# Softmax minus one-hot over 8192 rows: six in-place f32 row buffers, moved as two-row blocks in partition halves

## The chip, the core and the metric

The kernel runs on one core of one Trainium2 chip. The metric is the device time of one execution in microseconds. TensorE (PE) hardly takes part; the work is done by ScalarE (ACT), VectorE (DVE), a little by GpSimd (POOL), and by the core's 16 DMA engines, for which SyncE (SP) and ACT issue the large transfers.

## The reference

For each of 8 x 1024 = 8192 rows of 8192 logits: the softmax, from which 1 is taken away at the row's label.

```python
logits_max = np.max(logits, axis=-1, keepdims=True)
exp_logits = np.exp(logits - logits_max)
softmax = exp_logits / np.sum(exp_logits, axis=-1, keepdims=True)
one_hot[batch_idx, seq_idx, labels] = 1.0
return (softmax - one_hot).astype(np.float32)
```

Logits and result are f32, 268.4 MB each, so 537 MB cross between HBM and SBUF. The labels reach the kernel as 8-byte integers.

## The kernel before, in words

The rows are cut into 64 tiles of 128 rows, one row in each partition: 32 KB per partition, 4.194 MB per tile. The single loop runs over the tiles; the order of instructions on each engine follows the loop, and each instruction waits for its data by semaphores that the framework places.

Line 41 makes a constant of the column numbers 0 to 8191 as int16 on POOL. Then, for each tile:

- Line 47: SP issues the load of the tile into `logits_tile`. There are four such buffers, so the load of tile t has to wait until the store of tile t-4 has been read out of the same buffer.
- Line 50: POOL issues the load of the 128 labels, one per partition. Line 57: DVE turns them into f32.
- Line 61: ACT computes the exponential of the tile into `exp_bf` (bf16, two buffers). The row maximum isn't subtracted. The row sum is accumulated in the same pass.
- Line 71: DVE takes the reciprocal of the sum.
- Line 74: DVE compares the column numbers with the label and multiplies by the sum. The result, bf16, overwrites the first half of the logits' buffer.
- Line 83: DVE subtracts that from the exponentials.
- Line 85: DVE multiplies by the reciprocal and writes the f32 result over the tile's buffer.
- Line 87: ACT issues the store of the tile from that buffer.

Of the kernel before, what the change touches and what calls it, by code (L numbers as in the profile page):

```python
# [1 line left out]

# [4 lines left out]

P = 128


@with_exitstack
def kernel(
    ctx: ExitStack,
    tc: tile.TileContext,
    logits: bass.AP,
    labels: bass.AP,
    out: bass.AP,
):
    nc = tc.nc  # L20
    fp32 = mybir.dt.float32
    bf16 = mybir.dt.bfloat16
    i16 = mybir.dt.int16

    logits_nv = logits.flatten_outer_dims()
    out_nv = out.flatten_outer_dims()
    labels_n = labels
    while len(labels_n.shape) > 1:
        labels_n = labels_n.rearrange("a b ... -> (a b) ...")

    N, V = logits_nv.shape
    assert N % P == 0, f"N={N} must be a multiple of {P}"
    n_tiles = N // P

    const_pool = ctx.enter_context(tc.tile_pool(name="const", bufs=1))
    io_pool = ctx.enter_context(tc.tile_pool(name="io", bufs=4))
    work_pool = ctx.enter_context(tc.tile_pool(name="work", bufs=2))
    stats_pool = ctx.enter_context(tc.tile_pool(name="stats", bufs=4))

    iota_pv = const_pool.tile([P, V], i16)  # L40
    nc.gpsimd.iota(iota_pv[:, :], [[1, V]], channel_multiplier=0)  # L41

    for ti in range(n_tiles):
        rs = ti * P

        logits_tile = io_pool.tile([P, V], fp32, tag="io")
        nc.sync.dma_start(out=logits_tile[:], in_=logits_nv[rs : rs + P, :])  # L47

        labels_tile = stats_pool.tile([P, 1], labels_n.dtype, tag="labels")
        nc.gpsimd.dma_start(out=labels_tile[:], in_=labels_n[rs : rs + P, None])  # L50

        labels_f32 = stats_pool.tile([P, 1], fp32, tag="labels_f32")
        if mybir.dt.size(labels_n.dtype) == 8:
            labels_i32 = labels_tile.bitcast(mybir.dt.int32)[:, :1]
        else:
            labels_i32 = labels_tile[:]
        nc.vector.tensor_copy(out=labels_f32[:], in_=labels_i32)  # L57

        exp_bf = work_pool.tile([P, V], bf16, tag="exp")
        sum_f32 = stats_pool.tile([P, 1], fp32, tag="sum")  # L60
        nc.scalar.activation(  # L61
            out=exp_bf[:],
            in_=logits_tile[:],
            func=mybir.ActivationFunctionType.Exp,
            bias=0.0,
            scale=1.0,
            accum_out=sum_f32[:],
        )

        recip_sum = stats_pool.tile([P, 1], fp32, tag="recip")  # L70
        nc.vector.reciprocal(out=recip_sum[:], in_=sum_f32[:])  # L71

        ohts_bf = logits_tile.bitcast(bf16)[:, :V]
        nc.vector.tensor_scalar(  # L74
            out=ohts_bf,
            in0=iota_pv[:, :],
            scalar1=labels_f32[:],
            scalar2=sum_f32[:],
            op0=mybir.AluOpType.is_equal,
            op1=mybir.AluOpType.mult,  # L80
        )

        nc.vector.tensor_sub(out=exp_bf[:], in0=exp_bf[:], in1=ohts_bf)  # L83

        nc.vector.tensor_scalar_mul(out=logits_tile[:], in0=exp_bf[:], scalar1=recip_sum[:])  # L85

        nc.scalar.dma_start(out=out_nv[rs : rs + P, :], in_=logits_tile[:])  # L87


# [1 line left out]
_INS = ['logits', 'labels']  # L91
_OUTS = [((8, 1024, 8192), 'float32')]


# [23 lines left out]
```

## Time and profile before

| | us |
|---|---|
| median of 8 runs | 1255.51 |
| lowest and highest | 1254.31, 1257.36 |
| the profiled execution | 1257.36 |
| its span in the profile | 1255.5 |
| DVE busy | 732.6 |
| ACT busy | 457.0 |
| POOL busy | 253.0 |
| load, median from issue to landing | 29.1 |
| store, median from issue to landing | 29.4 |

The span runs from the first instruction to the last event that the profile holds. Busy time is the time in which an engine executes an instruction; the issuing of a DMA is not counted in it, so SP has none. "SPq" and "ACTq" name an engine's sequencer as it issues DMAs. In the groups of instructions, the part before the bar gives the operation, what it writes and reads with the shapes, and how often; after the bar stand the total busy time in us, the mean of one in ns, and the idle time of the engine just before these instructions with what ended it. Landing is the moment at which a transfer's completion is signalled.

### The profile page before, as it was taken

How to read it: one execution, taken by the hardware profiler on the slowest of the kernel's cores; microseconds unless marked ns; L12 is line 12 of the kernel's file. 1: busy time of each engine (PE TensorE's matmuls, PEld its weight loads, DVE VectorE, ACT ScalarE, POOL GpSimd, SP SyncE). 2: the span in 40 equal slices, each digit the busy share in tenths (PEclk: the TensorE clock that was granted, in tenths of full speed). 3: DMA queues.
4: the chain of work that ended last, by engine and by line, in shares of the span. 5: the costliest groups of instructions: out<-in, count | busy, mean ns of one | idle time of the engine just before them, and what ended most of it. 6: DMA issues, size and time to landing. Idle time of an engine off the chain costs nothing.

```text
span 1255.5 us, 992 instructions
## 1 busy us (share of the span) xinstructions
DVE 732.6 (58%) x320; ACT 457.0 (36%) x129; POOL 253.0 (20%) x69
## 2 busy tenths in 40 slices
DVE  3764655646547456465564654746647556465573
ACT  4424244243342433424324334243342432423422
POOL 5312212212122121221221212212122122100000
DMA  9999999999999999999999999999999999999996
GB/s 399 421 431 434 434 434 433 432 434 433 433 432 428 433 434 433 434 433 433 430 434 432 434 433 426 434 434 434 433 433 432 433 433 433 432 432 430 432 434 276
DMA packets 20487, 537.01 MB, mean 428 GB/s; under 512 B 4096, under 2 KB 4096, under 8 KB 4096
## 3 DMA queue, kind: packets, MB, share of 16 engines
q1 hardware_dynamic: 9216, 268.44, 49.7%
q10 hardware_dynamic: 9216, 268.44, 49.5%
q0 software_dynamic: 2048, 0.07, 0.1%
q14 instruction: 7, 0.06, 0.0%
HBM read 268.50 MB, written 268.44 MB: 428 GB/s over the span
## 4 chain that ended last, share of the span: by engine, by line
DMA 73%; DVE 14%; issue 11%; POOL 1%; ACTq 1%; ACT 0%; SPq 0%; PEldq 0%
DMA logits_tile<-in_logits_dram 46%; DMA out_dram<-logits_tile 26%; DVE logits_tile L85 5%; DVE exp_bf L83 5%; DVE logits_tile L74 4%; DMA labels_tile<-in_labels_dram 1%; POOL iota_pv L41 1%; ACTq L87 1%; ACT exp_bf L61 0%; POOL labels_tile L50 0%; DVE recip_sum L71 0%; DVE labels_f L57 0%; ACTq L61 0%; SPq L47 0%; PEldq L113 0%
## 5 line engine op out<-in xcount | busy, mean ns | idle before, releaser
L61 ACT ACTIVATE exp_bf<-logits_tile 128x8192 bf16<-128x8192 f32 x64 | 449.8, 7029 | 774.2 <-DMA logits_tile<-in_logits_dram 760.7
L50 POOL DMA_DIRECT2D labels_tile<-in_labels_dram x64 | 245.9, 3843 | 834.8 <-DVE labels_f L57 832.8
L71 DVE RECIPROCAL recip_sum<-sum_f 128x1 f32<-128x1 f32 x64 | 10.5, 163 | 488.0 <-ACT exp_bf L61 488.0
L85 DVE TENSOR_SCALAR logits_tile<-exp_bf,recip_sum 128x8192 f32<-128x8192 bf16 x64 | 287.1, 4486 | 0.1
L83 DVE TENSOR_TENSOR exp_bf<-exp_bf,logits_tile 128x8192 bf16<-128x8192 bf16 x64 | 283.2, 4425 | 2.2
L74 DVE TENSOR_SCALAR logits_tile<-iota_pv,labels_f,sum_f 128x8192 bf16<-128x8192 int16 x64 | 154.3, 2411 | 0.3 <-issue 0.3
L57 DVE CAST labels_f<-labels_tile 128x1 f32<-128x1 int32 x64 | 9.4, 147 | 20.2 <-DMA labels_tile<-in_labels_dram 20.2
L61 ACT ACTIVATION_READ_ACCUMULATOR exp_bf<-logits_tile 128x1 f32 x64 | 11.9, 186 | 0.0
L41 POOL IOTA iota_pv<- 128x8192 int16 x1 | 6.9, 6943 | 0.4 <-PEq L113 0.4
L61 ACT ACT_TABLE_LOAD x1 | 1.3, 1283 | 0.7 <-PEq L102 0.7
L102 POOL MEMSET const-float32-0.0<- 128x1 f32 x1 | 0.1, 99 | 0.2 <-issue 0.2
L102 POOL MEMSET const-bfloat16-1.0<- 128x1 bf16 x1 | 0.1, 102 | 0.0
L102 POOL MEMSET const-uint8-127<- 128x1 uint8 x1 | 0.1, 102 | 0.0
L102 POOL MEMSET const-float32-1.0<- 128x1 f32 x1 | 0.1, 99 | 0.0
## 6 DMA issues: line engine op xcount, KB each, us to landing
logits_tile<-in_logits_dram SPq DMA_DIRECT2D x64, 4096.0 KB, 29.1
out_dram<-logits_tile ACTq DMA_DIRECT2D x64, 4096.0 KB, 29.4
labels_tile<-in_labels_dram POOLq DMA_DIRECT2D x64, 1.0 KB, 12.8
```

The lines of the kernel that those rows point to most:

```text
L41: nc.gpsimd.iota(iota_pv[:, :], [[1, V]], channel_multiplier=0)
L50: nc.gpsimd.dma_start(out=labels_tile[:], in_=labels_n[rs : rs + P, None])
L57: nc.vector.tensor_copy(out=labels_f32[:], in_=labels_i32)
L61: nc.scalar.activation(out=exp_bf[:], in_=logits_tile[:], func=mybir.ActivationFunctionType.Exp, bias=0.0, scale=1.0, accum_out=sum_f32[:],)
L71: nc.vector.reciprocal(out=recip_sum[:], in_=sum_f32[:])
L74: nc.vector.tensor_scalar(out=ohts_bf, in0=iota_pv[:, :], scalar1=labels_f32[:], scalar2=sum_f32[:], op0=mybir.AluOpType.is_equal, op1=myb ...
L83: nc.vector.tensor_sub(out=exp_bf[:], in0=exp_bf[:], in1=ohts_bf)
L85: nc.vector.tensor_scalar_mul(out=logits_tile[:], in0=exp_bf[:], scalar1=recip_sum[:])
L87: nc.scalar.dma_start(out=out_nv[rs : rs + P, :], in_=logits_tile[:])
L102: nc = _bacc.Bacc("TRN2", target_bir_lowering=False, num_devices=1)
```

## The change

All six row buffers are one f32 tile `X` of three slots with two rows each. A block is 256 rows; partition p holds the rows 2p and 2p+1 of it, which lie next to each other in HBM, so that 64 KB per partition are one run. `rows` moves one of the two rows of all 128 partitions (32 KB each); `halves` moves both rows of 64 partitions (64 KB each). Both kinds have 4.194 MB. Loads of the blocks 0 to 4 and 27 to 31 and stores of the blocks 0, 1 and 24 to 31 go by rows, the others by halves.

The arithmetic stays in place in `X`: DVE finds the negated row maximum, ACT writes the exponential in f32 over the logits with the maximum as its bias, DVE takes the reciprocal of the sum, ACT scales the row by it, and DVE compares the column numbers with the label and subtracts, in one pass. The bf16 buffers are gone. The column numbers are made by POOL in the last row buffer and copied by DVE to PSUM. All labels are loaded at once, converted, and transposed by PE so that each partition has its own.

The order is written out by hand (`manual_schedule`): each engine runs its instructions as the text has them. For row t that is: exponential of t (ACT), reciprocal of t (DVE), load of the next block where t+1 opens one (SP), maximum of t+1 (DVE), store of t-1 (issued by ACT), scaling of t (ACT), subtraction of t (DVE). The last row's scaling and subtraction are cut into two column halves.

The diff, cut to its core:

```diff
+SLOTS = 3
+G = 2
+Q = P // 2
...
+    lab_bp = labels.rearrange("a b -> (a b)").rearrange("(b q) -> b q", q=G * P)
+    x_b = x_nv.rearrange("(b p j) v -> b p j v", p=P, j=G)
+    o_b = o_nv.rearrange("(b p j) v -> b p j v", p=P, j=G)
...
+    X = const.tile([P, SLOTS, G, V], fp32)
+    rows = [(slice(0, P), slice(j, j + 1)) for j in range(G)]
+    halves = [(slice(0, Q), slice(0, G)), (slice(Q, P), slice(0, G))]
...
+    nc.scalar.dma_start(out=lab_raw[:], in_=lab_bp)
...
+    nc.vector.tensor_copy(out=lab_f[:], in_=lab32[:, :, :, 0])
...
+            nc.tensor.transpose(out=lab_ps[:, j, :], in_=lab_f[:, j, :], identity=ident[:])
+        nc.vector.tensor_copy(out=lab[:], in_=lab_ps[:])
...
+    made = X[:, SLOTS - 1, G - 1, :].bitcast(i16)[:, :V]
+    nc.gpsimd.iota(made, [[1, V]], base=0, channel_multiplier=0)
+    nc.vector.tensor_scalar(
+        out=iota[:].bitcast(i32), in0=made.bitcast(i32), scalar1=0, scalar2=None, op0=Alu.bitwise_or
+    )
...
+    def parts(b, head, tail):
+        return rows if b < head or b >= B - tail else halves
+
+    def load(b):
+        for ps, js in parts(b, 5, 5):
+            nc.sync.dma_start(out=X[ps, b % SLOTS, js, :], in_=x_b[b, ps, js, :])
...
+    def row_max(t):
+        nc.vector.tensor_reduce(
+            out=m[:, t : t + 1], in_=row(t), axis=mybir.AxisListType.X, op=Alu.max, negate=True
         )
...
-        nc.vector.tensor_sub(out=exp_bf[:], in0=exp_bf[:], in1=ohts_bf)
+    def exponent(t):
+        nc.scalar.activation(
+            out=row(t), in_=row(t), func=Act.Exp, bias=m[:, t : t + 1], scale=1.0,
+            accum_out=s[:, t : t + 1],
+        )
...
-        nc.vector.tensor_scalar_mul(out=logits_tile[:], in0=exp_bf[:], scalar1=recip_sum[:])
+    def normalize(t, c):
+        x = row(t)[:, c]
+        nc.scalar.activation(out=x, in_=x, func=Act.Copy, bias=0.0, scale=r[:, t : t + 1])
...
+    def subtract(t, c):
+        x = row(t)[:, c]
+        nc.vector.scalar_tensor_tensor(
+            out=x, in0=iota[:, c], scalar=lab[:, t % G, t // G : t // G + 1], in1=x,
+            op0=Alu.is_equal, op1=Alu.subtract, reverse1=True,
+        )
...
+    def store(t):
+        b, j = divmod(t, G)
+        pieces = parts(b, 2, 8)
+        if pieces is rows:
+            pieces = rows[j : j + 1]
+        elif j < G - 1:
+            return
+        for ps, js in pieces:
+            nc.scalar.dma_start(out=o_b[b, ps, js, :], in_=X[ps, b % SLOTS, js, :])
...
+    load(0)
+    row_max(0)
+    for t in range(T):
+        exponent(t)
+        inverse(t)
+        if t + 1 < T:
+            if (t + 1) % G == 0:
+                load((t + 1) // G)
+            row_max(t + 1)
+        if t > 0:
+            store(t - 1)
...
+        for c in cols:
+            normalize(t, c)
+        for c in cols:
+            subtract(t, c)
+    store(T - 1)
```

## The prediction

> **What bounds the kernel now.** I read the page's slices first, then its queues and groups, then the waits, then the two ends.
>
> ```profile
> span 1255.5 us, 992 instructions
> DVE 732.6 (58%) x320; ACT 457.0 (36%) x129; POOL 253.0 (20%) x69
> DMA  9999999999999999999999999999999999999996
> ...
> q1 hardware_dynamic: 9216, 268.44, 49.7%
> q10 hardware_dynamic: 9216, 268.44, 49.5%
> ```
>
> No engine is above 58%, while the DMA engines are full in 39 of 40 slices. Loads (q1) and stores (q10) take half each. The windows of the trace give the rate and the two ends (columns: stretch, length, busy time of DVE, ACT, POOL, clock, DMA share, GB/s):
>
> ```profile
> 0.00:60.00 60.00, 32.12 (x19) 29.66 (x9) 23.26 (x16) 1.00 0.98 410
> 60.00:1200.00 1140.00, 672.96 (x293) 413.09 (x116) 229.76 (x54) 1.00 1.00 433
> 1200.00:1224.84 24.84, 16.07 (x6) 7.13 (x3) 0.00 (x0) 1.00 0.99 427
> 1224.84:1255.50 30.66, 11.41 (x4) 7.12 (x2) 0.00 (x0) 1.00 0.65 278
> ```
>
> I take 433.5 GB/s for the middle (the page's slices say 432 to 434). A tile of 4.194 MB then takes 9.68 us, and 128 of them (64 in, 64 out) 1239 us. The remaining 16.5 us are the start (410 instead of 433.5 over 60 us: 3 us), the end (278 over 30.7 us: 11 us) and small dips. So only some 16 us can be won while the bytes stay the same; much more can be lost.
>
> The waits of the loading queue say what a load waits for, and the groups what an operation costs:
>
> ```profile
> SPq L47 <- DMA out_dram<-logits_tile: 1170.1, 60, 50.1
> ```
> ```profile
> L61 ACT ACTIVATE exp_bf<-logits_tile 128x8192 bf16<-128x8192 f32 x64 | 449.8, 7029 | 774.2 <-DMA logits_tile<-in_logits_dram 760.7
> L71 DVE RECIPROCAL recip_sum<-sum_f 128x1 f32<-128x1 f32 x64 | 10.5, 163 | 488.0 <-ACT exp_bf L61 488.0
> L83 DVE TENSOR_TENSOR exp_bf<-exp_bf,logits_tile 128x8192 bf16<-128x8192 bf16 x64 | 283.2, 4425 | 2.2
> ```
>
> 60 of 64 loads wait for a store to free their buffer. ACT waits for loads, DVE for ACT. The ends, in order of time:
>
> ```profile
> 13.14 7.03 ACT L61 ACTIVATE exp_bf<-logits_tile 128x8192 bf16<-128x8192 f32 x1 [11.12 <-DMA logits_tile<-in_logits_dram]
> ...
> 23.35 7.03 ACT L61 ACTIVATE exp_bf<-logits_tile 128x8192 bf16<-128x8192 f32 x1 [3.09 <-DMA logits_tile<-in_logits_dram]
> ```
> ```profile
> 1238.98 4.49 DVE L85 TENSOR_SCALAR logits_tile<-exp_bf,recip_sum 128x8192 f32<-128x8192 bf16 x1
> 1243.50 0.34 ACTq L87 DMA_DIRECT2D out_dram<-logits_tile  x1
> ```
>
> The first tile lands at 13.1. The last store is issued at 1243.5 and the span ends 12.0 us later: 9.7 us of bytes and **2.3 us fixed** per transfer.
>
> **What the Trainium skill says.**
> - "SBUF — State Buffer", Door 1: DMA bandwidth depends on how many of 16 ports the partitions reach; partitions 0 to 63 reach eight (196 GB/s measured there for 1 MiB, asymptote about 218; all 128 reach sixteen). All transfers of the trace before span 128 partitions, so it doesn't test this; its 433.5 fits sixteen ports.
> - "DMA: Bandwidth & Descriptors", rules for kernel authors: transfers to two partition halves serialize. Not tested here either.
> - "VectorE: DVE Perf Modes", tier table and errata: an fp32 two-source operation and a reduction run at one element per cycle, (N+151)/0.96 ns. The trace agrees where it can: L83, at two per cycle, should be (4096+151)/0.96 = 4424 ns; it is 4425.
>
> **The change, part by part** (R a row tile, B a block of two rows).
>
> *Engine work.* Out go L74, L83 and L85 (11.3 us of DVE per tile), L57 and 64 label DMAs on POOL. Per row come a maximum and a compare-subtract on DVE, each (8192+151)/0.96 = 8.69 us by the price above (PSUM as a source could add some 0.1), and L71's 0.16: 17.55 us, 64 times 1123 us, 88% of a span. ACT has an exponential (L61's 7.03 plus the 0.18 readout, 7.3 with a tensor as bias) and a scaling copy of about 7.1: 14.4 us, 922 in all. A row of DMA pairs takes 19.35 us, so neither engine is the bound: they hide under DMA by 1.8 us per row, and show at the ends.
>
> *Set-up.* The labels' DMA, conversion, two transposes and the iota's copy to PSUM stand ahead of the first maximum on DVE. POOL's iota is 6.9 us (L41); the copy is 4096 words, about 4.4 us: ready near 13, when row 0 lands. Cost 0 to 2 us on DVE, hidden since DMA has six free rows to load. ACT's small load ahead of the big ones: under 0.5 us.
>
> *Order of issue.* On DVE, the subtraction of t stands behind the maximum of t+1. In half mode, a block's store therefore goes out only after the next block's landing L: 8.69 + 8.69 + 0.1 = 17.5 us later. The store's wait sits on ACT ahead of the scaling of t; ACT is free at 16.1, waits 1.4 us and has the copy done by 25.4, just before DVE asks for it (26.2): covered by 0.8 us; without the cover that is what DVE would lose.
>
> *Half mode* is what decides: blocks 5 to 26 are loaded and 2 to 23 stored as halves of 64 partitions, 4.194 MB each. With three slots, load b+2 needs the slot of store b-1, half for half. From the landing of b to that of b+2: 17.5 (store issued) + 2.3 + h (first half stored) + 0.1 + 2.3 + 2h (two halves loaded in sequence) = 22.2 + 3h, two periods long. At 218 GB/s, h = 19.24, so a period is **40.0 us**. The DMA sum alone would be 4 x 9.68 = 38.7; equality is at h = 18.4 (228 GB/s). h isn't in the trace. Bounds: 9.68 (no limit, then the period is 38.7, no less as the sum binds) and 21.4 (196 GB/s, period 43.2). I take 19.24, because the fixed part is already counted.
>
> *Walk.* Row 0 lands at 13.1; maximum to 21.8, exponential to 29.1, then DVE runs on: subtraction of t ends at 46.7 + 17.55t. DMA is full with 10 row loads and 4 row stores (135.5 us + 2.7 of start) to about 137. The store of block 2 goes out at 134.5, alone; load 5 may start when its first half lands: 134.5+2.3+19.2 = 156, and lands at 156.1+2.3+38.5 = **197**. Load 6 follows in the queue: 235.4. Then pairs of 79.9: L26 = 235.4 + 10 x 79.9 = **1034.6**. From there all is in rows: 10 loads and 14.7 row stores remain, 24.7 x 9.68 = 239 us + 0.7 for the receipt: **1274**. DVE gives 1270 for the same end (subtractions every 17.55 from 1052, the last row in halves, 12.0 for its store), so DMA is late and DVE next.
>
> Span 1274 against 1255.5: +18.5. The profiled execution took 1257.36, 1.86 more than its span and 1.85 above the median of 1255.51; so that execution would become 1276, and the median **1274**.
>
> **The rivals.**
> 1. *The port limit doesn't bite, and DMA stays full.* For it: 433.5 GB/s is reached with both directions mixed, and half loads and half stores overlap most of the time. Against: 3 us of each direction per period run alone, and the skill's figure. If a half runs at 228 GB/s or more, the period is 38.7. Then 1239 + 3 (start) + 2 (the gap near 135) + the end. After the last landing stand maximum 8.7, subtraction 8.7, half a copy 3.7, two half subtractions 8.9 and the store 12.0, 42.7 us with gaps, before 30.7; waiting stores fill 29 to 39 of it, so 4 to 14 are lost: 1248 to 1258, likeliest **1250**: faster. It decides from 228 GB/s per half upward.
> 2. *The halves wait for more than their half*, or two DMA engines on one port get in each other's way so that directions don't overlap. If a load's half waits for both halves of the store, the loop is 22.2 + 4h, a period of 49.6: 21 x 9.6 = 202 more, **1476**. For it: all six rows are one tile. Against: load and store divide it alike.
> 3. *DVE becomes the bound.* Needs over 19.35 us per row against 17.55; each operation would have to be 0.9 us longer. 64 x 19.5 + 29 = 1277: folded into my case.
>
> **How the numbers follow.** My case, with h from 18.8 to 21.4 us: 0.52, from 1262 to 1274 + 21 x 3.2 = 1341. Rival 1: 0.30, of which 0.21 faster, 0.08 within 0.2% (1253 to 1258), 0.01 slower. Rival 2 and like trouble: 0.18, above the range. Range 1247 to 1341; the likeliest case's own 1262 to 1341. Measurement tells 0.2% from no change. Faster 0.21, same 0.08, slower 0.71.
>
> **What would show it.** DVE at 1120 to 1135 us busy, groups of 8.7 us; half transfers of about 21 us or more from issue to landing when alone, and a slice near 140 to 160 us at about 218 GB/s; 415 to 420 GB/s between 200 and 1030 us; ACT and DVE idle on loads, SP's queue on stores; rows at the end at 433. Wrong: 433 GB/s throughout the middle, or a slice in which one half alone moves faster than 230.

## The result, and the profile after

The changed kernel takes **1699.74 us** (median of 11 runs, 1689.49 to 1733.11) against 1255.32 for the kernel before: 1.353 times as long, 95% interval 1.351 to 1.356. The run of 1733.11 us, over 1.5% above the fastest, counts as slow; ratio and interval are of the fast runs alone. The forecast was 1274, with a range up to 1341: the sign was right, the size far off. The profiled execution has a span of 1710.4 us.

First the page's slices and queues of the changed kernel:

```profile
span 1710.4 us, 746 instructions
...
DMA  9999999999999999999999999999999999999998
GB/s 408 428 431 303 284 279 276 290 264 265 317 253 282 296 302 268 279 279 285 268 285 282 291 280 299 291 280 280 297 277 285 293 274 273 403 431 435 433 432 379
...
q1 hardware_dynamic: 6400, 268.44, 57.3%
q10 hardware_dynamic: 6448, 268.51, 41.7%
```

Both kernels show a row of nines for the DMA engines. But the line below it says that full engines now move some 280 GB/s in slices 4 to 34, where they moved 433 before. The slices at both ends, where everything goes by rows, are as fast as ever. So the DMA engines hardly lack work; their packets take longer. The page also says how much longer. A packet is one run, the contiguous bytes of one partition: by 20 loads in rows (2560 packets of 32 KB), 44 loads in halves (2816 of 64 KB) and 16 completions per transfer, q1's 6400 packets are accounted for. 57.3% of 16 x 1710.4 us is 15,681 us; 2560 row packets at 1.22 us (before: 49.7% of 16 x 1255.5 over 8192) take 3,120; the rest over 2816 is **4.46 us per 64 KB load packet, where two row packets take 2.44**. The same sum for the stores gives **2.95 us**. Together 7.41 us for 2 x 64 KB, on 16 engines 283 GB/s.

The windows of the same trace (columns: stretch, length, busy time of PE twice, DVE, ACT and POOL, then clock, DMA share, GB/s) set the stretches apart:

```profile
0.00:140.00 140.00, 0.39 (x2) 0.28 (x2) 124.92 (x24) 99.90 (x22) 7.43 (x7) 1.00 1.00 420
140.00:200.00 60.00, 0.00 (x0) 0.00 (x0) 45.43 (x9) 44.63 (x10) 0.00 (x0) 1.00 1.02 283
200.00:1400.00 1200.00, 0.00 (x0) 0.00 (x0) 695.89 (x120) 571.80 (x120) 0.00 (x0) 1.00 0.99 282
1500.00:1600.00 100.00, 0.00 (x0) 0.00 (x0) 100.00 (x19) 82.37 (x17) 0.00 (x0) 1.00 1.00 434
```

The fall comes soon after 140 us; the first store in halves was issued at 133.37. In the middle DVE is busy 58% of the time. The groups and waits:

```profile
L94 DVE TENSOR_REDUCE m<-X 128x1 f32<-128x8192 f32 x64 | 555.2, 8674 | 491.3 <-DMA X<-in_logits_dram 491.3
L99 ACT ACTIVATE X<-X,m 128x8192 f32<-128x8192 f32 x64 | 455.5, 7118 | 557.8 <-DVE m L94 557.8
L113 DVE SCALAR_TENSOR_TENSOR X<-iota,lab,X 128x8192 f32<-128x8192 int16 (+1 forms) x65 | 559.7, 8612 | 71.3 <-ACT X L109 71.3
L109 ACT ACTIVATE X<-X,r 128x8192 f32<-128x8192 f32 (+1 forms) x65 | 456.0, 7016 | 202.3 <-issue 129.7
```

The work that was added costs what it was said to cost (8.67 us for a maximum, 8.74 for a full-width subtraction in the timeline, 7.12 for a copy). DVE waits 491 us for loads, in 26 places.

### The profile page after: what moved, and what is told of

Read it like the earlier page. It is cut to its first block, busy times and chain, and to the rows that moved or that the text cites. A ratio compares the mean times of both kernels' runs of the same rounds, so it can differ in the third digit from the quotient of the medians.

```text
span 1710.4 us, 746 instructions
## 1 busy us (share of the span) xinstructions
PE 0.4 (0%) x2; PEld 0.3 (0%) x2; DVE 1118.1 (65%) x196; ACT 917.2 (54%) x194; POOL 7.4 (0%) x7
## 3 DMA queue, kind: packets, MB, share of 16 engines
q1 hardware_dynamic: 6400, 268.44, 57.3%
## 4 chain that ended last, share of the span: by engine, by line
DMA 52%; DVE 26%; another core or an unknown queue 19%; issue 1%; ACT 1%; SPq 0%; DVEq 0%; PE 0%; ACTq 0%
DMA out_dram<-X 26%; DMA X<-in_logits_dram 25%; DVE m L94 13%; DVE X L113 12%; ACT X L99 0%; DMA lab_raw<-in_labels_dram 0%; SPq L88 0%; DVE iota L76 0%; DVEq L174 0%; ACT X L109 0%; DVE r L105 0%; DVE lab_f L62 0%; DVEq L94 0%; PE lab_ps L67 0%
## 5 line engine op out<-in xcount | busy, mean ns | idle before, releaser
L94 DVE TENSOR_REDUCE m<-X 128x1 f32<-128x8192 f32 x64 | 555.2, 8674 | 491.3 <-DMA X<-in_logits_dram 491.3
L99 ACT ACTIVATE X<-X,m 128x8192 f32<-128x8192 f32 x64 | 455.5, 7118 | 557.8 <-DVE m L94 557.8
L113 DVE SCALAR_TENSOR_TENSOR X<-iota,lab,X 128x8192 f32<-128x8192 int16 (+1 forms) x65 | 559.7, 8612 | 71.3 <-ACT X L109 71.3
L109 ACT ACTIVATE X<-X,r 128x8192 f32<-128x8192 f32 (+1 forms) x65 | 456.0, 7016 | 202.3 <-issue 129.7
L105 DVE RECIPROCAL r<-s 128x1 f32<-128x1 f32 x64 | 9.7, 152 | 7.3 <-ACT X L99 7.3
L99 ACT ACTIVATION_READ_ACCUMULATOR X<-X,m 128x1 f32 x64 | 11.9, 187 | 0.0
L75 POOL IOTA X<- 128x8192 int16 x1 | 6.9, 6943 | 0.0
L76 DVE TENSOR_SCALAR iota<-X 128x4096 int32<-128x4096 int32 x1 | 4.4, 4427 | 0.1
```

Source lines behind the costliest of these rows:

```text
L75: nc.gpsimd.iota(made, [[1, V]], base=0, channel_multiplier=0)
L76: nc.vector.tensor_scalar(out=iota[:].bitcast(i32), in0=made.bitcast(i32), scalar1=0, scalar2=None, op0=Alu.bitwise_or)
L94: nc.vector.tensor_reduce(out=m[:, t : t + 1], in_=row(t), axis=mybir.AxisListType.X, op=Alu.max, negate=True)
L99: nc.scalar.activation(out=row(t), in_=row(t), func=Act.Exp, bias=m[:, t : t + 1], scale=1.0, accum_out=s[:, t : t + 1],)
L105: nc.vector.reciprocal(out=r[:, t : t + 1], in_=s[:, t : t + 1])
L109: nc.scalar.activation(out=x, in_=x, func=Act.Copy, bias=0.0, scale=r[:, t : t + 1])
```

## Experiments

Three theories were open. The **port theory** takes up the ports that the prediction cites: partitions 0 to 63 lie behind eight of sixteen, two DMA engines share one, and when both move the same way each gets half. The **run-length theory**: a 64 KB run is slow by itself. The **loop theory**: three slots keep the DMA short of work.

### Transfers alone

These kernels compute nothing; each stage loads into or stores from `X`, and a tiny DVE write to every buffer (`gap`) parts the stages. Each was run once. Two of the twelve stages; `LO` is partitions 0 to 63, `MID` 32 to 95, both in 64 KB runs:

```diff
...
+    for slot in range(SLOTS):
+        load(LO, slot)
+    gap()
+    for slot in range(SLOTS):
+        load(MID, slot)
+    gap()
...
```

> Transfers alone, no arithmetic: twelve stages of loads and stores of 64 partitions or 128, with a gap after each; nothing is computed, so the output is only data moved from the logits. Port theory (partitions 0 to 63 lie behind eight of the sixteen ports, so two DMA engines share one): loads of 0 to 63 alone at 215 to 218 GB/s, of 32 to 95, with the same bytes and the same 64 KB runs, at about 430; halves in turn on one queue 218, on two queues between 218 and 430; stores likewise; load beside store of halves 260 to 300 in all, of 32 to 95 about 433. Run-length theory (a 64 KB run is slow by itself): 0 to 63 and 32 to 95 and the 128-partition blocks are all equally slow, at 280 or below, and only the 32 KB rows reach 430. Loop theory (the three slots starve the DMA): every stage here is at 400 or above, since nothing waits.

The gaps in the timeline of this run part the stages. The wait in brackets before a gap is the length of its stage (the first load was issued at 0.73, so the first stage took 60.7):

```profile
61.42 0.06 DVE L66 MEMSET X<- 128x6 f32 x1 [61.42 <-DMA X<-in_logits_dram]
122.14 0.06 DVE L66 MEMSET X<- 128x6 f32 x1 [60.66 <-DMA X<-in_logits_dram]
186.21 0.06 DVE L66 MEMSET X<- 128x6 f32 x1 [64.01 <-DMA X<-in_logits_dram]
218.27 0.06 DVE L66 MEMSET X<- 128x6 f32 x1 [32.00 <-DMA X<-in_logits_dram]
342.91 0.06 DVE L66 MEMSET X<- 128x6 f32 x1 [124.58 <-DMA X<-in_logits_dram]
...
463.40 0.06 DVE L66 MEMSET X<- 128x6 f32 x1 [120.43 <-DMA X<-in_logits_dram]
```

Below, the prediction's 2.3 us are taken off each length for what isn't bytes.

| stage | MB | us | GB/s |
|---|---|---|---|
| loads, rows of all partitions | 25.2 | 60.7 | 431 |
| loads, 64 KB runs, all partitions | 25.2 | 60.7 | 431 |
| loads, 0 to 63 | 12.6 | 64.0 | 204 |
| loads, 32 to 95 | 12.6 | 32.0 | 424 |
| loads, both halves in turn, one queue | 25.2 | 124.6 | 206 |
| loads, both halves at once, two queues | 25.2 | 120.4 | 213 |
| stores, 0 to 63 | 12.6 | 63.2 | 207 |
| stores, 32 to 95 | 12.6 | 31.0 | 438 |
| load 0 to 63 beside store 64 to 127 | 25.2 | 89.5 | 289 |
| load beside store, both 0 to 63 | 16.8 | 61.1 | 285 |
| load beside store, both 32 to 95 | 16.8 | 52.4 | 335 |
| load beside store, rows of all partitions | 33.6 | 81.1 | 426 |

The third and fourth lines decide: same bytes, same number of partitions, same runs, each transfer one contiguous stretch of HBM, and a factor of two from where the partitions lie. It isn't the number of engines at work either: the DMA share is full in both stages.

```profile
125.00:183.00 58.00, 0.00 (x0) 0.00 (x0) 1.00 0.97 199
190.00:216.00 26.00, 0.00 (x0) 0.00 (x0) 1.00 1.02 444
```

Two more lines say how it works. Both halves at once on two queues reach all ports between them, and still get 213 GB/s. In this stage's trace (344 to 461 us) all packets in flight belong to one of the two queues for 82% of the time: the engines go through both queues in step, most of the time all on one half, then all on the other. And load beside store gives 285 to 289 GB/s, more than the 204 of one direction, and whether the two use the same half or opposite ones makes no difference. So directions that differ get in each other's way less than transfers in the same direction. How much less can't be read against the 426 of the last line: 32 to 95, without shared ports, gave 335 beside a store, where 433 was expected. The halves alone came out a little below the expected 215 to 218.

A second run of this kind:

> Transfers alone again, eleven stages with a gap after each; nothing is computed, the output is only data moved. Port theory (engines that share a port and move the same way each get half of it): loads of partitions 0 to 63 in 32 KB rows at 205 to 215 GB/s as with 64 KB; every second partition at 215 to 430, as the two engines that meet on a port stay together or not; 0 to 31 at about 200; 0 to 15 (four engines on one port) at about 105; 64 KB blocks of all partitions, load beside store, 425 to 435; 32 to 95 load beside store in 64 KB 430 if the 335 of the first look came from its short stage, below 390 if something else is shared there; 0 to 63 load beside store in 32 KB rows again 260 to 310; halves in loads alone beside blocks in stores about 290 while both run, halves in stores alone 290 to 390. Run-length theory: the 32 KB stages are the fast ones.

Loads of 0 to 63 in 32 KB rows took 64.0 us for 12.6 MB (204 GB/s), of every second partition 32.0 us (424), of 0 to 31 33.0 us for 6.3 MB (205), of 0 to 15 21.3 us for 2.1 MB (110). So the number of partitions doesn't set the rate: 16, 32, 64 and again 64 partitions give 110, 205, 204 and 424, which fits the ports. Load beside store of 64 KB blocks of all partitions gave only 338 (101.5 us for 33.6 MB), of 32 to 95 in 64 KB 336, in 32 KB rows 395, of 0 to 63 in 32 KB rows 305. Halves in loads alone, beside whole blocks in stores, gave 322 GB/s, halves in stores alone 365. The 338 and 336 were not foreseen, and led to a third run:

> Loads beside stores alone, no arithmetic, all data only moved; runs cut to 64, 32, 8 and 2 KB on the HBM side, first for all partitions, then (32, 8, 2 KB) for 0 to 63, then every second partition in 64 KB runs. If the length of a run sets what two directions on one engine cost each other: all partitions 338 to 350 GB/s at 64 KB and 425 or more at 32 KB and below, also inside one 8.4 MB transfer. If the size of the transfer does it: about 345 at every length. Partitions 0 to 63, port theory: 285 to 310 at every length if engines hand over only between runs, nearer to 400 if short runs let the two directions slide past each other. Every second partition: about 335 to 350, as for all partitions in 64 KB runs.

All partitions, load beside store, 33.6 MB: 99.8 us at 64 KB, 82.9 at 32, 82.3 at 8, 85.6 at 2 KB (344, 416, 419 and 403 GB/s): the size of the transfer was the same, so it is the run's length. Partitions 0 to 63, 16.8 MB: 57.0 us at 32 KB, 50.9 at 8, 49.3 at 2 KB (307, 345, 357): at each of these lengths well below all partitions, so shorter runs soften the collision and don't end it. Every second partition at 64 KB: 52.9 us (332).

### All by rows

```diff
-        return rows if b < head or b >= B - tail else halves
+        return rows
```

> All transfers by rows of 128 partitions, everything else as in the changed kernel. Port theory and run-length theory: 1246 to 1258 us, the middle back at 433 GB/s. Loop theory: six single rows wait for less than three blocks, so faster than 1700, but with a middle between 300 and 430 GB/s.

Measured: **1248.0 us**, 0.9944 of the kernel before (0.9927 to 0.9961), as expected, and a little less than both kernels. The rest of the change, arithmetic and six buffers, is worth 7 us; the whole loss is in the halves. The windows and queues of this run show where the 7 us are:

```profile
140.00:1100.00 960.00, 0.00 (x0) 0.00 (x0) 880.06 (x152) 724.91 (x153) 0.00 (x0) 1.00 1.00 433
...
1220.00:1230.00 10.00, 0.00 (x0) 0.00 (x0) 8.87 (x2) 4.41 (x2) 0.00 (x0) 1.00 1.02 439
1230.00:1240.00 10.00, 0.00 (x0) 0.00 (x0) 0.00 (x0) 0.00 (x0) 0.00 (x0) 1.00 1.01 436
```
```profile
q1 hardware_dynamic: 9216, 268.44, 50.0%
q10 hardware_dynamic: 9264, 268.51, 49.9%
```

The middle is where it was. But after the last arithmetic there are stores waiting that keep the engines full to 1240 us, where the kernel before ran its last 30.7 us at 278.

### Every second partition instead of partition halves

```diff
-    halves = [(slice(0, Q), slice(0, G)), (slice(Q, P), slice(0, G))]
+    halves = [(slice(0, P, 2), slice(0, G)), (slice(1, P, 2), slice(0, G))]
```

> The halves are every second partition in place of 0 to 63 and 64 to 127: same number of transfers, same bytes, same 64 KB runs, same waits, but each half reaches all ports. Port theory: most of the loss is gone, what stays is what 64 KB runs lose when both directions run (338 to 400 GB/s in the middle): 1300 to 1440 us. Loop theory and plain run-length theory: 1690 or more as before.

Measured: **1275.72 us**, ratio 1.017 (1.015 to 1.020), below the range that the port theory was given. 424 of the 444 us are gone, and the edit is the choice of partitions alone. It also changes which rows of HBM a half holds, but that is no rival: 0 to 63 and 32 to 95 above were both contiguous, and differed by a factor of two. The loop and run-length theories fall as explanations of the loss. The middle and the queues:

```profile
200.00:1020.00 820.00, 0.00 (x0) 0.00 (x0) 718.70 (x125) 586.82 (x124) 0.00 (x0) 1.00 1.00 420
```
```profile
q1 hardware_dynamic: 6400, 268.44, 50.6%
q10 hardware_dynamic: 6448, 268.51, 48.8%
```

By the same sum as above a 64 KB packet takes 2.56 us (load) and 2.43 (store), which makes 420 GB/s, and the engines are full. This run is 28 us longer than rows alone. That is mostly not engines waiting in the loop: 2816 load packets, each 0.12 us longer, are some 20 us on 16 engines (an estimate from these packet times), and the shares of the queues leave about 6 us more idle than by rows. The timeline shows the first half-loaded block, and the landings two blocks apart in the middle:

```profile
197.18 8.69 DVE L94 TENSOR_REDUCE m<-X 128x1 f32<-128x8192 f32 x1 [9.82 <-DMA X<-in_logits_dram]
```
```profile
594.04 8.69 DVE L94 TENSOR_REDUCE m<-X 128x1 f32<-128x8192 f32 x1 [6.80 <-DMA X<-in_logits_dram]
...
674.93 8.69 DVE L94 TENSOR_REDUCE m<-X 128x1 f32<-128x8192 f32 x1 [7.68 <-DMA X<-in_logits_dram]
...
755.97 8.69 DVE L94 TENSOR_REDUCE m<-X 128x1 f32<-128x8192 f32 x1 [8.11 <-DMA X<-in_logits_dram]
```

197 was forecast, and 79.9 for two periods: they are 80.9 and 81.0. Why this match proves little is said below.

### One direction by halves

```diff
-        pieces = parts(b, 2, 8)
+        pieces = rows
```

> Loads by halves as in the changed kernel, stores all by rows. Port theory: the two engines of a port collide only in their loads, so about half of the loss or somewhat more: 1400 to 1600 us. Run-length theory: the 64 KB loads alone are slow, 1450 to 1500. Loop theory: stores leave row by row and earlier, so under 1350.

Measured: 1668.15 us (ratio 1.327, 1.322 to 1.332), above what any theory said. The counterpart, stores alone in halves:

```diff
-        for ps, js in parts(b, 5, 5):
+        for ps, js in rows:
```

> Stores by halves as in the changed kernel, loads all by rows. Port theory, if stores collide as loads do: a 64 KB store takes twice as long, 7.2 us for a load and a store on an engine, about 1640 us. If they collide as seldom as in the changed kernel, where a 64 KB store took 2.95 us against 4.46 for a load: 5.4 us, a period of 43 us, about 1340 us. Loop theory: the stores of whole blocks are what starves the loads, so nearly all of the loss is here, over 1600.

Measured: 1596.77 us (1.273, 1.271 to 1.275). Either direction alone costs most of the loss (413 and 342 us of 444), so the two losses don't add. The packets say more. By the same sum as for the changed kernel, in us for 64 KB:

| | load | store | sum | GB/s from the sum | in the windows |
|---|---|---|---|---|---|
| changed kernel | 4.46 | 2.95 | 7.41 | 283 | 282 |
| loads by halves | 4.57 | 2.53 | 7.10 | 295 | 297 |
| stores by halves | 2.55 | 4.14 | 6.69 | 313 | 315 |
| every second partition | 2.56 | 2.43 | 4.99 | 420 | 420 |

Where one direction alone is in halves, its packets take 1.7 to 1.9 times their normal 2.44; in the stages of that direction alone above they took 5.10, against 2.45 for 32 to 95. So they collide most of the time. While such a packet ran, 13 of the 16 packets in flight went its way on the average. In the changed kernel the loads collide nearly as much and the stores much less. There, too, a load packet was slower the more of the others were loads: 2.8 us where fewer than 4 of the packets in flight were loads on the average, 5.0 where nearly all were; for stores the same comparison gives only 2.7 and 3.6. The estimate for stores alone by the 2.95 of the changed kernel (1340 us) was therefore wrong, the one for full collision (1640) nearer. The loop theory's "over 1600" was nearer still, but that theory is ruled out by the run with every second partition. Why the two directions divide the collision so unevenly isn't settled.

### Half of the bytes on all ports

```diff
-    halves = [(slice(0, Q), slice(0, G)), (slice(Q, P), slice(0, G))]
+    halves = [(slice(32, 96), slice(0, G)), (slice(0, 32), slice(0, G)), (slice(96, P), slice(0, G))]
```

> In place of the halves 0 to 63 and 64 to 127 three pieces: 32 to 95 (one engine per port), 0 to 31 and 96 to 127 (two engines per port); same bytes, same 64 KB runs, one transfer more per block. Port theory: half of the bytes collide, half don't, so about half to two thirds of the loss is gone: 1420 to 1560 us. Loop or run-length theory: no better than 1690.

Measured: 1563.22 us (1.240, 1.232 to 1.249; 1560.2 without the longest of the four, 1587.45): at the upper edge of the range of the port theory and far from the others. Three tenths of the loss are gone with half of the bytes moved off the shared ports, 319 GB/s in the middle.

### Whole blocks

```diff
-    halves = [(slice(0, Q), slice(0, G)), (slice(Q, P), slice(0, G))]
+    halves = [(slice(0, P), slice(0, G))]
```

> In place of two halves one transfer of both rows of all 128 partitions, 8.4 MB in 64 KB runs. Port theory: full rate while transfers run, but a load now waits for a whole store, which makes a period of about 41 us instead of 38.7: 1290 to 1320 us. Run-length theory: about as slow as the halves, 1650 or more. Loop theory: slower than the halves, over 1700.

The second run has this edit, and places the rows p and p+128 of a block in partition p, so that the runs are 32 KB (the stores and the labels are changed to match):

```diff
-    x_b = x_nv.rearrange("(b p j) v -> b p j v", p=P, j=G)
...
+    x_b = x_nv.rearrange("(b j p) v -> b p j v", p=P, j=G)
...
```

> Whole blocks of 8.4 MB as in the run with one transfer of both rows of all 128 partitions, but with rows p and p+128 in a partition, so that the runs are 32 KB. If the 64 KB run costs something by itself: the loop alone stays, a period near 41 us, 1295 to 1310. If the wait for whole blocks was the whole loss: 1325 to 1335 as with 64 KB runs.

Measured: 1332.06 us with 64 KB runs (1.061, 1.060 to 1.063) and 1326.35 with 32 KB (1.057, 1.055 to 1.059). The first is above the 1290 to 1320 of the port theory, the second within the range given for the wait alone. Every transfer reaches all partitions, and 368 and 373 of the loss's 444 us are gone. But a load now waits for a whole store. With 64 KB runs:

```profile
140.00:1080.00 940.00, 0.00 (x0) 0.00 (x0) 771.16 (x134) 636.90 (x134) 0.00 (x0) 1.00 0.95 395
```

A DMA share of 0.95 and 395 GB/s make a period of 42.5 us instead of 38.7; with 32 KB runs they are 0.96 and 399. Here engines do lack work. The run's length is worth 6 us of 1332, so the 344 GB/s of the transfers alone doesn't carry over to a kernel whose directions run side by side only part of the time, or out of step; which of the two wasn't tried.

## Why the prediction was wrong

**The step that failed** is the size of h: "At 218 GB/s, h = 19.24, so a period is **40.0 us**." It took the rate of a half that moves alone, and let loads and stores have that rate at the same time. The same is in its DMA sum of a period, 4 x 9.68 = 38.7 us, which has halves overlap at the full rate. Loads beside stores in halves reach 285 to 289 GB/s together, not 2 x 218. The landings in the changed kernel's trace show what came of it; these are the first and the last half-loaded block:

```profile
227.75 8.69 DVE L94 TENSOR_REDUCE m<-X 128x1 f32<-128x8192 f32 x1 [41.77 <-DMA X<-in_logits_dram]
...
1466.48 8.69 DVE L94 TENSOR_REDUCE m<-X 128x1 f32<-128x8192 f32 x1 [20.77 <-DMA X<-in_logits_dram]
```

The first landed at 227.75 instead of 197, 31 us late. In the middle the landings are 58.6 us apart on the average (block 15 at 825.29, block 25 at 1410.98). Four transfers of 4.194 MB in 58.6 us are 286 GB/s, the rate of loads beside stores, and the engines are full (share 0.99): so it is the DMA sum that binds, at 58.6 us instead of 38.7. Put into the prediction's own formula, two periods of 117.1 give h = (117.1 - 22.2)/3 = 31.6 us instead of 19.24, far outside its bounds of 9.68 and 21.4. The last half-loaded block landed at 1466.48 instead of 1034.6: 432 of the 436 us between the forecast span of 1274 and the 1710.4.

The upper bound was the mistake in method: 196 GB/s is a price for a half that moves by itself, and the trace of the kernel before has no transfer of a half at all. The other extreme is that the two directions take turns: some 217 GB/s for both together (half of 433.5), an estimated period of 77 us. It belonged into the range.

**The rivals.** The second named the cause in half a sentence ("two DMA engines on one port get in each other's way so that directions don't overlap") and then priced another mechanism, the wait for both halves, at 1476 us. Its direction was right, with a chance of 0.18; its price was too low, and the directions do overlap in part (285 against 204 to 207 alone). That other mechanism isn't what made the loss: with every second partition, the same waits give 1275.72. The first rival (the limit doesn't bite: 1250) is refuted for the halves, while its sum comes out for rows: 1248.0.

The prediction's own sign for its case, 415 to 420 GB/s in the middle, didn't come: 282.

**What held.**
- The floor of 1239 us: rows alone come to 1248, so some 7 of the 16 us that could be won were won.
- Maximum and subtraction 8.69 each: 8.67 and 8.74; DVE 1118 us busy against 1123; the copy to PSUM 4.43 against 4.4.
- The walk up to the first half: row 0 was expected at 13.1 and its maximum began at 13.42; the first half store was issued at 133.37 against 134.5. (135.5 + 2.7 in the walk is 138, not 137; nothing rests on it.)
- The end in rows at full rate: 434 GB/s between 1500 and 1600 us.

**A match by luck.** With every second partition the landing at 197.18, the two periods of 81 us and the span of 1274.4 fit the forecast. They don't confirm it. Its 19.24 us per half came from a rate of 218 GB/s, and such a half, loaded alone, moves at 424. The prediction's own case for halves without that limit is the first rival, 1248 to 1258: 18 us too low at the least. The formula gives h = 19.6 here because load and store share the engines: 4.194 MB at half of 420 GB/s are 20.0 us (an estimate).

**The rules that the prediction cited.** The Trainium skill's "SBUF — State Buffer", Door 1, by which bandwidth depends on how many ports the partitions reach, fits the runs in one direction: 204 GB/s for 0 to 63, 205 for 0 to 31, 110 for 0 to 15. The rule of its "DMA: Bandwidth & Descriptors", rules for kernel authors, that transfers to two partition halves serialize fits too: 213 GB/s for loads of both at once. Neither page gives a rate for a half that is loaded beside a store, and that decided here. The prediction's price of (N+151)/0.96 ns stands in "VectorE: DVE Perf Modes", errata, for an fp32 `tensor_tensor`; that it also holds for the maximum and the subtraction was its own step, and came out (8.67 and 8.74 us against 8.69).

**The 0.8 us of cover** on ACT was wrong in a way that cost nothing, as far as the waits show. A store by rows took ACT 0.34 to 0.38 us to issue. Two half stores in a row took several us, as here, in order of time:

```profile
900.08 5.82 ACTq L126 DMA_DIRECT2D out_dram<-X  x2
905.95 7.12 ACT L109 ACTIVATE X<-X,r 128x8192 f32<-128x8192 f32 x1 [7.31 <-issue]
...
913.11 8.75 DVE L113 SCALAR_TENSOR_TENSOR X<-iota,lab,X 128x8192 f32<-128x8192 int16 x1 [4.40 <-ACT X L109]
...
942.11 8.69 DVE L94 TENSOR_REDUCE m<-X 128x1 f32<-128x8192 f32 x1 [20.19 <-DMA X<-in_logits_dram]
```

The copy starts late and DVE loses 4.4 us, but afterwards it waits 20.2 us for the next load all the same: the slower loads left room for it.

## What to carry to other kernels

A DMA queue that is busy is not a DMA queue at its rate: read GB/s beside the share, and divide a queue's time by its packets. Cut a transfer so that every piece moves at the full rate (rows of all partitions, or every second partition, not partitions 0 to 63); here that choice alone was 424 us. A run that hits a forecast's number confirms it only if it has the forecast's terms. When a price is known for one direction alone, put the case of no overlap with the other direction into the range.

## What was not expected of the hardware

- Two queues that load opposite halves at the same time get hardly more (213 GB/s) than one queue that loads them in turn (206).
- Every second partition of 128 moves at 424 GB/s in loads alone, nearly as fast per byte as all of them (431).
- With all partitions, 64 KB runs lose nothing in one direction (431 GB/s, as 32 KB rows do), but load beside store they fell to 338 and 344 in two stages, against 416 at 32 KB; in the whole kernel 64 KB instead of 32 KB runs cost 6 us. The cause is open.
- The issue of a single half store held ACT for up to 6.67 us in the changed kernel, 3.39 with every second partition and 2.69 with stores alone in halves, against 0.34 to 0.38 for stores by rows. Slow stores as such aren't the cause, since with every second partition they aren't slow; what is stays open.
